# A mixture-of-experts layer: expert weights in three 1-MB loads into pair buffers instead of six 512-KB loads

## The chip, the cores and the metric

The kernel runs on one core of a Trainium2 chip. The metric is the device time of one execution in microseconds (us); shorter is better. Five engines work side by side, each through its own instructions in the order in which the program lists them: TensorE (PE, matrix products), VectorE (DVE), ScalarE (ACT), GpSimd (POOL) and SyncE (SP, which here issues loads and stores). They wait for one another by semaphores. 16 DMA engines move the data.

## The reference, cut to what matters

One layer of an encoder over 1088 tokens (1024 of a prompt and 64 of samples), width 1024: latent attention and a gated convolution, a projection added to the residual, a mixture of 32 experts with the top two of a chosen group, and a gated embedding.

```python
x = x + m @ w_o
h2 = rmsnorm(x, g_ffn).reshape(B * S, D)
# hier_moe: group by top 1 of 4, experts by top 2 of 8 in the group; for each block of tokens of expert eid:
a = xblk @ w1[eid]                       # w1, w3: 1024 x 256 for each expert
b = xblk @ w3[eid]
return (jax.nn.silu(a) * b) @ w2[eid]    # w2: 256 x 1024
...
x = x + hier_moe(h2, ...)
x = x + sigmoid(rmsnorm(x, g_ple) @ w_pg) * (p @ w_ple)
```

All of it is float32. The kernel makes each product from three: an operand is split into a rounded high part and the rest, and high x high, low x high and high x low are summed (`mm3`, lines 64, 65 and 66).

## The kernel before

Up to 740 us run the projections, attention and the convolution; to 860 us the output projection and the router, during which the weights of experts 0 to 4 are fetched. From 860 to about 1192 us stands the **expert stage**. For each of the 32 experts in turn:

- its up to 96 tokens are gathered from `h2d` (L1363, issued by POOL, three experts ahead);
- `x_tr` transposes them on PE (L1373, two banks of four 128-column pieces, 8 instructions), ACT casts the high part `xTh` (one per bank) and DVE makes the low part `xTl`;
- `w13_mm` multiplies by w1 and w3: 24 matmuls of 512 columns (8 pieces of the width, three terms each), called **W** of the expert below;
- `act_` takes the silu on ACT (`sa`, L1391) and the product on DVE (L1392); `a_tr` transposes it with 2 PE instructions (L1399); ACT casts `ath`, DVE makes `atl`;
- `w2_mm` multiplies by w2 in two halves of the width: 12 matmuls, called **Y**; ACT copies each half out (`y`, L1416, two copies); a scatter writes them (L1419).

The weights of an expert lie in memory as six tiles of 128 x 1024 (four of w1 and w3, two of w2). Each is split: ACT casts the high part `weh` (L58), DVE subtracts for the low part `wel` (L61), six of each in flight. So ACT and DVE have six splits per expert, beside the small steps above.

The loads are issued by SP (`e_load`, `w_dma`, L954). Each load is 512 KB with rows of 4 KB, into one of 30 slots of its own; five experts fit, and the load of expert e + 6 is issued behind expert e. A load is held until the load five before it has landed (`DEEP`). Behind the last expert's weights follow `pT` and `wple` (the embedding) and `wpg` (the gate), by the same function.

In the expert stage the order of POOL and SP is the order of the code. The order of PE, DVE and ACT is picked by a scheduler when the program is built: it plays the code through with its own estimates of when an operand will be there, those of the loads among them. Behind the experts come four `ple` products, a loop for experts with more tokens than fit (not entered with this data), and a last stage that PE fills, to the end.

Of the kernel before, what the change touches and what calls it, by code (L numbers as in the profile page):

```python
# [7 lines left out]
F32 = mybir.dt.float32  # L8
# [24 lines left out]
NOV = 22  # L33
NOROW = 2200.0
A2 = 2 * T
DEEP = 5
WARM = 10
WARM0 = 14

# [2 lines left out]
def body(ctx, tc, a):  # L42
# [894 lines left out]
    fxs, fx = opened("flex")  # L937
    NHL, NY = 6, 3

    def slot(j, shape, dt, name):  # L940
        return (fx if j < 24 else fx2[0]).tile(shape, dt, name=name, tag=f"fx{j}", bufs=1)

    fx2 = []
    EP = ((0, 1), (2, 3), (8, 9), (6, 7), (4, 5))

    MCH = ((0, 384), (384, 384), (768, 320))
    mT = [[slot(3 * (2 * (i // 3) + s) + i % 3, [128, KD, 128], F32R, f"mT{i}{s}") for s in range(2 - (i == 8))]
          for i in range(NT)]
    eraw, wsl = {}, {}

    wdma = []
# [6 lines left out]
                              reason="bounded queue")  # L958
        wdma.append(r.ins)

    def e_load(e, js=range(6)):
        for j in js:
            r = slot(3 * EP[e % len(EP)][j // 3] + j % 3, [128, 1024], F32, "eraw")
            w_dma(r, a["we"][e, j])
            eraw[e, j] = r

    ys, yp = opened("ya", bufs=2)
    aTh, aTl = [], []
# [47 lines left out]
    mcf = lgp.tile([128, 32], BF16, name="mcf")  # L1016
    trib = lgp.tile([128, 128], BF16, name="trib")
    oneb = lgp.tile([128, 128], BF16, name="oneb")
    nc.vector.memset(oneb, 1.0)
    nc.vector.memset(lg[:, NT - 1], 0.0)  # L1020
    was, wap = opened("woA", side="right")
    wo = {}
    wos = {k: slot(q, [128, 2, 512], F32R, "wos") for k, q in ((0, 18), (1, 19), (2, 20), (3, 21), (4, 22), (5, 23), (7, 17))}

    def wo_get(k):
        wo[k] = []
# [235 lines left out]
    for i in range(6):  # L1262
        p = i - 1
        o_mm(i, 0, {} if i == 0 else {
            **({0: [(route3, i - 2)]} if i >= 2 else {}), 1: [(o_tr, p, 1), (o_h2, p)], 4: [(o_rt, p, 0, 4)],
            5: [(o_rt, p, 4, 8)], 7: [(o_lg, p), (route1, p)]})
        o_add(i, 0)
        if 1 <= i:
            o_load(i + 1)
        if i == 5:  # L1270
            o_load(7)
        if i == 0:
            e_load(2, range(3))
        if i == 1:
            e_load(2, range(3, 6))
        if i >= 1:
            e_load((i - 1) // 3, ((i - 1) % 3, 3 + (i - 1) % 3))
        o_mm(i, 1, {**({5: [(route2, p)]} if i >= 1 else {}), 6: [(o_tr, i, 0)]})
        o_add(i, 1)
        o_sq(i)  # L1280
# [1 line left out]
                7: [(o_lg, 5), (route1, 5)]})  # L1282
    o_add(6, 0)
    o_load(8)
    e_load(1, (2, 5))
# [5 lines left out]
    e_load(4, (2,))  # L1291
# [4 lines left out]
    e_load(4, (0, 3))  # L1296
# [4 lines left out]
    e_load(4, (5,))  # L1301
# [12 lines left out]
    wpx = {}  # L1314

    def wpx_get(q):
        if q not in wpx:
            wpx[q] = slot(9 + q, [128, 1024], F32R, "wpx")
        return wpx[q]

    def e_hi(e, j):
        if e == NE and j >= NHL:
# [22 lines left out]
        e_hi(e, j)  # L1345
        e_lo(e, j)

    e_load(4, (1, 4))
    route1(7)
    for j in range(6):  # L1350
        e_hi(0, j)
# [141 lines left out]
    for j in range(2, 6):  # L1493
# [4 lines left out]

    PL = {}
    plo = {}  # L1500
    XS = ((2, 5, 8), (20, None, None), (0, 1, 6), (7, 3, 4), (21, 22, 23), (18, 19, None), (2, 5, 8), (20, None, None),
          (0, 1, 6))

    def pl_load(j):
        for k in range(2):
            PL["r", j, k] = slot((24, 27)[j] + k, [128, 1024], F32, "plr")
            w_dma(PL["r", j, k], a[("pT", "wple")[j]][:, k, 0:1024])
        if j == 0:
            PL["r8"] = slot(26, [128, 2, 64], F32, "plr8")
            w_dma(PL["r8"], a["pT"][:, :, NP:])  # L1510

    def pl_split(j, k):
        h = PL["h", j, k] = slot((21, 3)[j] + k, [128, 1024], F32R, "plh")
        l = PL["l", j, k] = slot((0, 6)[j] + k, [128, 1024], F32R, "pll")
        r = PL["r", j, k]
        hi(h, r)
        lo(l, r, h[:])
        if j == k == 0:
            t = PL["c8"] = slot(23, [128, 2, 128], F32R, "plc8")
            hi(t[:, :, 0:64], PL["r8"])  # L1520
            lo(t[:, :, 64:128], PL["r8"], t[:, :, 0:64])
# [88 lines left out]
    with tc.For_i(0, nov, 1) as i:  # L1610
        ev = nc.values_load(ovi[0:1, bass.ds(i + 1, 1)], engines=(mybir.EngineType.SP,), min_val=0, max_val=NE - 1,
                            skip_runtime_bounds_check_because="bounded by a minimum on the chip")
        xgo = op_.tile([128, D], F32, name="xgo", tag="xyo")
        nc.gpsimd.memset(xgo, 0.0)
        rb = op_.tile([128, 128], F32, name="rb")
        V_.tensor_scalar(out=rb, in0=rid, scalar1=bs, scalar2=None, op0=OP.add)
        V_.tensor_scalar(out=bs, in0=bs, scalar1=128.0, scalar2=None, op0=OP.add)
        ps = bank()
        for k in range(2):
            for t in range(NT):  # L1620
                am = op_.tile([128, 128], F32, name="amo", bufs=1)
# [141 lines left out]
def pack(inp):  # L1763
# [107 lines left out]
```

## Time and profile before

| what | value |
|---|---|
| median of 3 runs | 1332.31 us (1332.3 to 1336.3) |
| the profiled execution | 1331.4 us, its span 1329.5 us |
| PE busy | 1268.9 us, 95% of the span |
| DVE busy | 854.9 us, 64% |
| ACT busy | 650.6 us, 49% |
| weights' DMA queue (q1) | 221.86 MB, 47.8% of 16 engines' span |
| the four experts in 1067 to 1106 us | 39.0 us, 9.75 us for each |

The first time is a whole execution's, the span runs from the first to the last instruction; the rest of the table is of the span. A busy share is a mean over stages with different limits: how an engine stands in one stage is read from a window of that stage. PE works through its instructions in order, so a wait on PE delays all behind it; a busy ACT or DVE delays PE only where the row that PE needs stands behind others in their queues.

### The profile page before, as it was taken

How to read it: one execution, taken by the hardware profiler on the slowest of the kernel's cores; microseconds unless marked ns; L12 is line 12 of the kernel's file. 1: busy time of each engine (PE TensorE's matmuls, PEld its weight loads, DVE VectorE, ACT ScalarE, POOL GpSimd, SP SyncE). 2: the span in 40 equal slices, each digit the busy share in tenths (PEclk: the TensorE clock that was granted, in tenths of full speed). 3: DMA queues.
4: the chain of work that ended last, by engine and by line, in shares of the span. 5: the costliest groups of instructions: out<-in, count | busy, mean ns of one | idle time of the engine just before them, and what ended most of it. 6: DMA issues, size and time to landing. Idle time of an engine off the chain costs nothing. (4 is left out here: it accounts for less than half of the span.)

```text
span 1329.5 us, 20478 instructions
## 1 busy us (share of the span) xinstructions
PE 1268.9 (95%) x7255; PEld 1100.2 (83%) x7255; DVE 854.9 (64%) x1652; ACT 650.6 (49%) x1278; POOL 319.4 (24%) x376
## 2 busy tenths in 40 slices
PE   9999999999988999999999999789999999999998
PEld 8999999999978988888998887556766666667886
DVE  6433354336684566766559755689888888884743
ACT  6311242223344455655545211358888888785322
POOL 2000011125653233433315200032222222210310
PEclk9999999999998999999999999989999999999999
DMA  7111398535665524332357755799999999947511
GB/s 271 57 48 48 136 365 307 195 116 165 148 204 189 168 74 135 89 131 74 97 187 264 263 195 213 249 295 358 357 354 349 348 351 343 352 173 279 198 40 56
DMA packets 106777, 273.94 MB, mean 206 GB/s; under 512 B 13729, under 2 KB 42897, under 8 KB 106642
## 3 DMA queue, kind: packets, MB, share of 16 engines
q1 hardware_dynamic: 90544, 221.86, 47.8%
q0 software_dynamic: 15840, 50.68, 11.9%
q8 instruction: 58, 0.95, 0.3%
q14 instruction: 45, 0.37, 0.1%
q10 hardware_dynamic: 290, 0.07, 0.0%
HBM read 212.72 MB, written 67.19 MB: 211 GB/s over the span
## 5 line engine op out<-in xcount | busy, mean ns | idle before, releaser
L61 DVE TENSOR_TENSOR wel<-eraw,weh 128x1024 fp32r<-128x1024 f32 x192 | 228.5, 1220 | 35.6 <-ACT weh L58 33.8
L58 ACT CAST weh<-eraw 128x1024 fp32r<-128x1024 f32 x192 | 195.5, 1054 | 10.9 <-PE bk L66 10.9
L829 POOL TENSOR_TENSOR P<-P,ri 128x128 f32<-128x128 f32 (+8 forms) x72 | 77.2, 1077 | 128.5 <-DVE ri L828 108.9
L65 PE MATMUL bk<-wel,xTh 128*96 128x512 f32 x256 | 103.6, 405 | 2.0 <-DVE wel L61 1.7
L64 PE MATMUL bk<-weh,xTh 128*96 128x512 f32 x256 | 102.3, 400 | 2.4 <-ACT xTh L58 1.7
L66 PE MATMUL bk<-weh,xTl 128*96 128x512 f32 x256 | 102.6, 401 | 0.0
L1419 POOL DMA_INDIRECT Yd<-y,idx x32 | 41.0, 1280 | 234.0 <-ACT y L1416 215.5
L64 PE MATMUL bk<-hTAh,wh 128*128 128x384 f32 x224 | 76.3, 341 | 0.5 <-ACT hTAh L257 0.3
L65 PE MATMUL bk<-hTAl,wh 128*128 128x384 f32 x224 | 76.1, 340 | 0.0
L66 PE MATMUL bk<-hTAh,wl 128*128 128x384 f32 x224 | 75.9, 339 | 0.0
L64 PE MATMUL fg<-hTBh,fw 128*128 128x384 f32 (+1 forms) x224 | 74.5, 333 | 0.3 <-ACT fgm L665 0.2
L66 PE MATMUL fg<-hTBh,fw 128*128 128x384 f32 (+1 forms) x224 | 72.9, 326 | 0.0
L65 PE MATMUL fg<-hTBl,fw 128*128 128x384 f32 (+1 forms) x224 | 72.7, 325 | 0.0
L58 ACT CAST wh<-w_r 128x1024 fp32r<-128x1024 f32 x28 | 29.4, 1051 | 87.5 <-issue 42.4
L64 PE MATMUL bk<-hTBh,wh 128*128 128x384 f32 (+1 forms) x192 | 62.0, 324 | 0.2 <-ACT hTBh L58 0.2
L65 PE MATMUL bk<-hTBl,wh 128*128 128x384 f32 (+1 forms) x192 | 62.0, 323 | 0.0
L66 PE MATMUL bk<-hTBh,wl 128*128 128x384 f32 (+1 forms) x192 | 61.9, 323 | 0.0
L61 DVE TENSOR_TENSOR wl<-w_r,wh 128x1024 fp32r<-128x1024 f32 x28 | 34.3, 1225 | 40.0 <-ACT wh L58 39.9
L65 PEld LDWEIGHTS bk<-wel,xTh 128*96 128x96 f32 x256 | 41.6, 163 | 22.2 <-DVE wel L61 7.9
L64 PE MATMUL bk<-weh,ath 128*96 128x512 f32 x128 | 51.0, 398 | 8.9 <-ACT ath L58 8.8
L815 DVE TENSOR_REDUCE nm<-S 128x1 f32<-128x128 f32 (+8 forms) x72 | 50.8, 706 | 12.3 <-PE S L66 11.2
L64 PEld LDWEIGHTS bk<-weh,xTh 128*96 128x96 f32 x256 | 41.5, 162 | 20.6 <-ACT xTh L58 3.1
(804 smaller groups left out, 3749.7 us busy)
## 6 DMA issues: line engine op xcount, KB each, us to landing
eraw<-in_we_dram SPq DMA_DIRECT2D x192, 512.0 KB
fw<-wsd POOLq DMA_DIRECT2D x32, 512.0 KB, 5.1
w_r<-in_wing_dram SPq DMA_DIRECT2D x28, 512.0 KB
gm_r<-gscr SPq DMA_DIRECT2D x16, 544.0 KB
wsd<-wh SPq DMA_DIRECT2D x16, 512.0 KB
wsd<-wl SPq DMA_DIRECT2D x16, 512.0 KB
xy<-Yd SPq DMA_DIRECT2D x16, 512.0 KB
vd<-V SPq DMA_DIRECT2D x10, 512.0 KB
```

Source lines behind the costliest of these rows:

```text
L58: nc.scalar.copy(dst, src)
L61: (eng or nc.vector).tensor_tensor(out=dst, in0=src, in1=h.bitcast(F32), op=OP.subtract)
L64: r = nc.tensor.matmul(ps, sh, mh, start=first, stop=False)
L65: nc.tensor.matmul(ps, sh, ml, start=False, stop=False)
L66: nc.tensor.matmul(ps, sl, mh, start=False, stop=last)
L815: nc.vector.tensor_reduce(out=nm, in_=s, axis=AX.XY, op=OP.max, negate=True)
L829: nc.gpsimd.tensor_tensor(out=P[:, :nk], in0=P[:, :nk], in1=ri.to_broadcast([128, nk]), op=OP.mult)
L1419: nc.gpsimd.indirect_dma_start(out=Yd[:, :], out_offset=bass.IndirectOffsetOnAxis(ap=col, axis=0), in_=buf, in_offset=None, bounds_check=A ...
```

## The change

The weights lie in memory as three tiles of 128 x 2048 per expert. A load is 1 MB with rows of 8 KB, into one of 15 pair buffers, which hold two of the former slots; the held-back load waits for the one three before it. The embedding's and the gate's weights are loaded as pairs too. The buffers that other stages borrow are renumbered accordingly, and a small tile (`plc8`) gets a place of its own. The number of instructions on PE, DVE, ACT and POOL stays the same; SP has 456 in place of 558.

```diff
-DEEP = 5
+DEEP = 3
...
-    def slot(j, shape, dt, name):
-        return (fx if j < 24 else fx2[0]).tile(shape, dt, name=name, tag=f"fx{j}", bufs=1)
...
-    EP = ((0, 1), (2, 3), (8, 9), (6, 7), (4, 5))
+    EP = ((0, 1, 2), (3, 4, 5), (12, 13, 14), (9, 10, 11), (6, 7, 8))
+
+    def pair(p, dt, name):
+        return (fx if p < 12 else fx2[0]).tile([128, 2, 1024], dt, name=name, tag=f"fx{p}", bufs=1)
...
-    def e_load(e, js=range(6)):
-        for j in js:
-            r = slot(3 * EP[e % len(EP)][j // 3] + j % 3, [128, 1024], F32, "eraw")
-            w_dma(r, a["we"][e, j])
-            eraw[e, j] = r
+    def e_load(e, qs=range(3)):
+        for q in qs:
+            r = pair(EP[e % len(EP)][q], F32, "eraw")
+            w_dma(r, a["we"][e, q].rearrange("p (j n) -> p j n", j=2))
+            for j in range(2):
+                eraw[e, 2 * q + j] = r[:, j]
...
-            e_load((i - 1) // 3, ((i - 1) % 3, 3 + (i - 1) % 3))
+            e_load((i - 1) // 3, ((i - 1) % 3,))
...
     def pl_load(j):
+        r = pair(12 + j, F32, "plr")
+        w_dma(r, a[("pT", "wple")[j]][:, :, 0:1024])
         for k in range(2):
-            PL["r", j, k] = slot((24, 27)[j] + k, [128, 1024], F32, "plr")
-            w_dma(PL["r", j, k], a[("pT", "wple")[j]][:, k, 0:1024])
+            PL["r", j, k] = r[:, k]
...
     def wpg_load(s):
-        for k in range(3 * s, min(3 * s + 3, KD)):
-            eraw[NE, k] = slot(12 + k, [128, 1024], F32, "eraw")
-            w_dma(eraw[NE, k], a["wpg"][:, k])
+        for q in range(*((0, 3), (3, 4))[s]):
+            r = pair((9, 10, 11, 6)[q], F32, "eraw")
+            w_dma(r, a["wpg"][:, 2 * q:2 * q + 2])
+            for j in range(2):
+                eraw[NE, 2 * q + j] = r[:, j]
...
-    A["we"] = np.ascontiguousarray(we.reshape(32, 128, 6, 1024).transpose(0, 2, 1, 3))
+    A["we"] = np.ascontiguousarray(we.reshape(32, 128, 3, 2048).transpose(0, 2, 1, 3))
```

Up to the W of expert 16 the rows of PE, DVE and ACT stand as before. From there on the scheduler picks another order, with a pattern that repeats every four experts in both kernels. Three places show it.

**ACT, from the splits of w2 of expert 20 on, before.** `weh_11940` and `weh_11968` are these splits, `weh_11987` and on of expert 21 (`weh<-eraw` is a split), `y_12011` is the output of expert 19, `xTh0_12039` and `xTh1_12068` are the casts of expert 21's tokens, `sa_12077` is the silu of expert 20:

```order
L58 CAST weh_11940<-eraw_11420 128x1024
L58 CAST weh_11968<-eraw_11422 128x1024
L58 CAST xTh0_12039<-bk_12041 128x384
L58 CAST weh_11987<-eraw_11524 128x1024
L1416 COPY y_12011<-bk_12012 96x512
L58 CAST weh_12031<-eraw_11526 128x1024
L1416 COPY y_12011<-bk_12020 96x512
L58 CAST weh_12035<-eraw_11528 128x1024
L58 CAST xTh1_12068<-bk_12070 128x384
L58 CAST weh_12048<-eraw_11530 128x1024
L1391 ACTIVATE sa_12077<-bk_11991 96x256
```

The first cast stands ahead of four splits and both copies of `y`. The same place now: `weh_11820` and the four behind it are expert 21's splits, `y_11844` the output of expert 19, `xTh0_11872` and `xTh1_11901` expert 21's tokens:

```order
L58 CAST weh_11820<-eraw_11387 128x1024
L58 CAST weh_11864<-eraw_11387 128x1024
L1394 ACTIVATE sa_11910<-bk_11824 96x256
L1419 COPY y_11844<-bk_11845 96x512
L58 CAST weh_11868<-eraw_11389 128x1024
L1419 COPY y_11844<-bk_11853 96x512
L58 CAST weh_11881<-eraw_11389 128x1024
L58 CAST xTh0_11872<-bk_11874 128x384
L58 CAST xTh1_11901<-bk_11903 128x384
L58 CAST ath_11940<-bk_11937 128x192
```

Both casts moved behind both copies of `y` and four splits of expert 21.

**PE at the W of expert 21, before.** `bk_12020` is the second half of Y of expert 19, `bk_12041` and `bk_12070` take the transposed tokens of expert 21, `bk_11991` is W of expert 20:

```order
L64 MATMUL bk_12012<-weh_11828,ath_12001 96x512
L65 MATMUL bk_12012<-wel_11829,ath_12001 96x512
L64 MATMUL bk_12020<-weh_11828,ath_12001 96x512
L65 MATMUL bk_12020<-wel_11829,ath_12001 96x512
L1373 MATMUL bk_12041<-ident_58,xg0_9662 128x96 x4
L1373 MATMUL bk_12070<-ident_58,xg0_9662 128x96 x4
L65 MATMUL bk_11991<-wel_11924,xTh1_11956 96x512
```

The transposes stand amid W of expert 20. There now (`bk_11853` is the second half of Y of expert 19, `bk_11874` and `bk_11903` the tokens of expert 21, `bk_11930` its W, `bk_11937` the transposed activations of expert 20, `bk_11951` its Y):

```order
L66 MATMUL bk_11853<-weh_11701,atl_11835 96x512
L1376 MATMUL bk_11874<-ident_58,xg0_9621 128x96 x4
L1376 MATMUL bk_11903<-ident_58,xg0_9621 128x96 x4
L64 MATMUL bk_11930<-weh_11820,xTh0_11872 96x512
L65 MATMUL bk_11930<-wel_11821,xTh0_11872 96x512
L1402 MATMUL bk_11937<-ident_58,sa_11910 128x96 x2
L64 MATMUL bk_11951<-weh_11779,ath_11940 96x512
L65 MATMUL bk_11951<-wel_11780,ath_11940 96x512
L64 MATMUL bk_11959<-weh_11779,ath_11940 96x512
```

Before, 19 more matmuls of PE (W of expert 20 and Y of expert 19) stand between these transposes and the W that needs their casts. Now none does.

**ACT behind the first copy for expert 22, now.** `y_11950` is the output of expert 20, `weh_11926` and on are splits of expert 22, `sa_12016` is the silu of expert 21, `xTh0_11978` and `xTh1_12007` are the casts of expert 22's tokens:

```order
L58 CAST weh_11926<-eraw_11493 128x1024
L1419 COPY y_11950<-bk_11951 96x512
L58 CAST weh_11970<-eraw_11493 128x1024
L1419 COPY y_11950<-bk_11959 96x512
L58 CAST weh_11974<-eraw_11495 128x1024
L58 CAST weh_11987<-eraw_11495 128x1024
L1394 ACTIVATE sa_12016<-bk_11930 96x256
L58 CAST xTh0_11978<-bk_11980 128x384
L58 CAST xTh1_12007<-bk_12009 128x384
```

The casts are the last two rows. Before (`weh_12099` and on are of expert 22, `xTh0_12151` the cast of its tokens, `y_12123` the output of expert 20):

```order
L58 CAST weh_12099<-eraw_11636 128x1024
L58 CAST weh_12143<-eraw_11638 128x1024
L58 CAST ath_12113<-bk_12110 128x192
L1391 ACTIVATE sa_12189<-bk_12103 96x256
L58 CAST xTh0_12151<-bk_12153 128x384
L58 CAST xTh1_12180<-bk_12182 128x384
L1416 COPY y_12123<-bk_12124 96x512
L58 CAST weh_12147<-eraw_11640 128x1024
L1416 COPY y_12123<-bk_12132 96x512
L58 CAST weh_12160<-eraw_11642 128x1024
```

Here, too, the casts moved behind the copies and three splits. On PE, the transposes of expert 22 are now ended right ahead of its W, with 4 matmuls of expert 21 between Y of expert 20 and them. For expert 23 PE has 4, 4, 2 and 4 instructions (W of expert 22, half of the transposes, W, the other half) between Y of expert 21 and the W, and ACT has `y`, split, `y`, split, `xTh0`. For expert 24, ACT has the casts ahead of the copies.

Toward the end, ACT now has the two splits of `pT` (`plh`) behind `ath` of expert 28; before, they stand behind the splits of expert 31:

```order
L58 CAST xTh1_12749<-bk_12751 128x384
L58 CAST ath_12779<-bk_12776 128x192
L58 CAST plh_12959<-plr_12553 128x1024 x2
L58 CAST weh_12733<-eraw_12239 128x1024
L58 CAST weh_12761<-eraw_12239 128x1024
L58 CAST plc8_7586<-late_12555 128x2x64
L58 CAST weh_12765<-eraw_12341 128x1024
L1419 COPY y_12789<-bk_12790 96x512
```

The two splits of `pT` stand ahead of the last two splits of expert 29.

## Rows read from the trace of the kernel before

**Rows 1.** Windows: us, busy of PE, PEld, DVE, ACT, POOL, clock, DMA share, GB/s.

```profile
1067.00:1106.00 39.00, 37.58 (x186) 26.29 (x185) 34.26 (x41) 32.58 (x49) 9.85 (x8) 1.00 1.00 347
1145.00:1203.00 58.00, 53.61 (x242) 37.03 (x240) 44.97 (x53) 47.23 (x68) 8.34 (x7) 1.00 0.60 209
```

**Rows 2.** What PE waited for in 1067 to 1106: us, times, longest us.

```profile
PE bk L64 <- ACT ath L58: 1.2, 1, 1.2
PE bk L64 <- ACT xTh L58: 0.2, 1, 0.2
```

**Rows 3.** Timeline of PE in 1085 to 1089: start us, us, engine, line, out<-in, [idle].

```profile
1085.31 0.82 PE L1373 MATMUL bk<-ident,xg 96*128 96x96 f32 x8
...
1086.38 0.47 PE L64 MATMUL bk<-weh,xTh 128*96 128x512 f32 x1 [0.24 <-ACT xTh L58]
...
1086.92 0.39 PE L66 MATMUL bk<-weh,atl 128*96 128x512 f32 x1
...
1088.77 0.33 PE L1399 MATMUL bk<-ident,sa 96*128 96x96 f32 x2
```

**Rows 4.** Timeline of ACT over the same stretch.

```profile
1085.84 0.86 ACT L58 CAST xTh<-bk 128x384 fp32r<-128x384 f32 x2 [1.31 <-PE bk L1373]
1088.04 0.58 ACT L1416 COPY y<-bk 96x512 f32<-96x512 f32 x1 [1.33 <-PE bk L66]
1088.52 1.05 ACT L58 CAST weh<-eraw 128x1024 fp32r<-128x1024 f32 x1
1089.47 0.58 ACT L1416 COPY y<-bk 96x512 f32<-96x512 f32 x1
1089.94 1.05 ACT L58 CAST weh<-eraw 128x1024 fp32r<-128x1024 f32 x1
```

**Rows 5.** Groups by line, 911 to 1106: busy us, mean ns, idle before.

```profile
L61 DVE TENSOR_TENSOR wel<-eraw,weh 128x1024 fp32r<-128x1024 f32 x121 | 144.0, 1221 | 23.7 <-ACT weh L58 22.7 <-DMA eraw<-in_we_dram 0.2
...
L61 DVE TENSOR_TENSOR xTl<-bk,xTh 128x384 fp32r<-128x384 f32 x40 | 20.7, 548 | 0.0
...
L1392 DVE TENSOR_TENSOR sa<-sa,bk 96x256 f32<-96x256 f32 x20 | 8.2, 408 | 0.0
...
L1391 ACT ACTIVATE sa<-bk 96x256 f32<-96x256 f32 x20 | 7.6, 380 | 0.0
```

**Rows 6.** What PE waited for in 1145 to 1203.

```profile
PE bk L65 <- DVE wel L61: 1.7, 3, 0.8
PE bk L1399 <- DVE sa L1392: 1.2, 1, 1.2
PE bk L64 <- ACT weh L58: 0.7, 2, 0.5
PE bk L64 <- ACT ath L58: 0.4, 1, 0.4
```

**Rows 7.** What PE waited for in 870 to 911.

```profile
PE bk L1373 <- DMA xg<-h2d,idx: 3.0, 2, 2.0
```

**Rows 8.** Timeline of POOL at the first gather.

```profile
865.73 1.14 POOL L1363 DMA_INDIRECT xg<-h2d,idx  x1 [5.30 <-DMA eraw<-in_we_dram]
```

**Rows 9.** DMA queues in 900 to 1150: packets, MB, share of 16 engines.

```profile
q1 hardware_dynamic: 20269, 73.83, 83.5%
```

**Rows 10.** Timeline of SP in 1150 to 1176.

```profile
1158.02 3.14 SPq L954 DMA_DIRECT2D plr<-in_pT_dram  x3
1161.92 2.33 SPq L954 DMA_DIRECT2D plr<-in_wple_dram  x2
1165.20 6.30 SPq L954 DMA_DIRECT2D eraw<-in_wpg_dram  x6
```

**Rows 11.** Timeline of ACT, DVE and PE at the loop after the experts.

```profile
1202.72 1.11 ACT L1536 COPY plo<-bk 128x512 f32<-128x512 f32 x2
...
1202.90 1.28 DVE L1338 SCALAR_TENSOR_TENSOR wel<-eraw,gplc,weh 128x1024 fp32r<-128x1024 f32 x1 [0.72 <-ACT weh L1330]
...
1205.08 0.80 PE L64 MATMUL bk<-plh 128*128 128x512 f32 x1 [2.14 <-DVEq L1610]
```

More of the change, by code (lines that the diff above doesn't have):

```diff
@@ L938, in body @@
     NHL, NY = 6, 3
-    def slot(j, shape, dt, name):
-        return (fx if j < 24 else fx2[0]).tile(shape, dt, name=name, tag=f"fx{j}", bufs=1)
     fx2 = []
-    EP = ((0, 1), (2, 3), (8, 9), (6, 7), (4, 5))
+    EP = ((0, 1, 2), (3, 4, 5), (12, 13, 14), (9, 10, 11), (6, 7, 8))
+    def pair(p, dt, name):
+        return (fx if p < 12 else fx2[0]).tile([128, 2, 1024], dt, name=name, tag=f"fx{p}", bufs=1)
     MCH = ((0, 384), (384, 384), (768, 320))
-    mT = [[slot(3 * (2 * (i // 3) + s) + i % 3, [128, KD, 128], F32R, f"mT{i}{s}") for s in range(2 - (i == 8))]
-          for i in range(NT)]
+    mTp = [pair(i, F32R, f"mT{i}") for i in range(NT)]
+    mT = [[mTp[i][:, q].rearrange("p (k n) -> p k n", k=KD) for q in range(2 - (i == 8))] for i in range(NT)]
     eraw, wsl = {}, {}
@@ L1018, in body @@
     oneb = lgp.tile([128, 128], BF16, name="oneb")
+    plc8 = lgp.tile([128, 2, 128], F32R, name="plc8")
     nc.vector.memset(oneb, 1.0)
@@ L1022, in body @@
     wo = {}
-    wos = {k: slot(q, [128, 2, 512], F32R, "wos") for k, q in ((0, 18), (1, 19), (2, 20), (3, 21), (4, 22), (5, 23), (7, 17))}
+    wosp = [pair(9 + q, F32R, "wos") for q in range(3)]
+    wos = {k: wosp[k // 2][:, k % 2].rearrange("p (s n) -> p s n", s=2) for k in range(6)}
+    wos[7] = mTp[8][:, 1].rearrange("p (s n) -> p s n", s=2)
     def wo_get(k):
@@ L1272, in body @@
         if i == 0:
-            e_load(2, range(3))
+            e_load(2, (0, 1))
         if i == 1:
-            e_load(2, range(3, 6))
+            e_load(2, (2,))
         if i >= 1:
-            e_load((i - 1) // 3, ((i - 1) % 3, 3 + (i - 1) % 3))
+            e_load((i - 1) // 3, ((i - 1) % 3,))
         o_mm(i, 1, {**({5: [(route2, p)]} if i >= 1 else {}), 6: [(o_tr, i, 0)]})
@@ L1284, in body @@
     o_load(8)
-    e_load(1, (2, 5))
+    e_load(1, (2,))
     o_mm(8, 0, {5: [(route2, 5)]})
@@ L1290, in body @@
     o_sq(8)
-    e_load(4, (2,))
     o_mm(6, 1, {1: [(o_tr, 8, 1), (o_h2, 8)], 3: [(o_rt, 8, 0, 8)], 4: [(o_lg, 8), (route1, 8)],
@@ L1295, in body @@
     o_sq(6)
-    e_load(4, (0, 3))
+    e_load(4, (0,))
     o_mm(7, 0, {0: [(o_tr, 6, 1)], 1: [(route2, 8), (o_h2, 6)], 2: [(o_rt, 6, 0, 8)], 3: [(route3, 8)],
@@ L1300, in body @@
     e_load(3)
-    e_load(4, (5,))
+    e_load(4, (2,))
     route1b(6)
@@ L1316, in wpx_get @@
     def wpx_get(q):
-        if q not in wpx:
-            wpx[q] = slot(9 + q, [128, 1024], F32R, "wpx")
-        return wpx[q]
+        if q // 2 not in wpx:
+            wpx[q // 2] = pair(9 + q // 2, F32R, "wpx")
+        return wpx[q // 2][:, q % 2]
     def e_hi(e, j):
@@ L1346, in e_split @@
         e_lo(e, j)
-    e_load(4, (1, 4))
+    e_load(4, (1,))
     route1(7)
@@ L1500, in body, with half @@
     plo = {}
-    XS = ((2, 5, 8), (20, None, None), (0, 1, 6), (7, 3, 4), (21, 22, 23), (18, 19, None), (2, 5, 8), (20, None, None),
-          (0, 1, 6))
+    XS = (((2, 0), (2, 1), (5, 1)), ((14, 1), None, None), ((0, 0), (0, 1), (1, 0)), ((1, 1), (7, 0), (7, 1)),
+          ((8, 0), (8, 1), (14, 0)), ((6, 0), (6, 1), None), ((2, 0), (2, 1), (5, 1)), ((14, 1), None, None),
+          ((0, 0), (0, 1), (1, 0)))
+    own = {}
+    def half(p, q):
+        if p not in own:
+            own[p] = pair(p, F32, "late")
+        return own[p][:, q]
     def pl_load(j):
+        r = pair(12 + j, F32, "plr")
+        w_dma(r, a[("pT", "wple")[j]][:, :, 0:1024])
         for k in range(2):
-            PL["r", j, k] = slot((24, 27)[j] + k, [128, 1024], F32, "plr")
-            w_dma(PL["r", j, k], a[("pT", "wple")[j]][:, k, 0:1024])
+            PL["r", j, k] = r[:, k]
         if j == 0:
-            PL["r8"] = slot(26, [128, 2, 64], F32, "plr8")
+            PL["r8"] = half(14, 0)[:, 0:128].rearrange("p (k n) -> p k n", k=2)
             w_dma(PL["r8"], a["pT"][:, :, NP:])
     def pl_split(j, k):
-        h = PL["h", j, k] = slot((21, 3)[j] + k, [128, 1024], F32R, "plh")
-        l = PL["l", j, k] = slot((0, 6)[j] + k, [128, 1024], F32R, "pll")
+        if k == 0:
+            PL["hl", j] = [pair((7, 0)[j] + q, F32R, "pl" + "hl"[q]) for q in range(2)]
+        h = PL["h", j, k] = PL["hl", j][0][:, k]
+        l = PL["l", j, k] = PL["hl", j][1][:, k]
         r = PL["r", j, k]
         hi(h, r)
-        lo(l, r, h[:])
+        lo(l, r, h)
         if j == k == 0:
-            t = PL["c8"] = slot(23, [128, 2, 128], F32R, "plc8")
+            t = PL["c8"] = plc8
             hi(t[:, :, 0:64], PL["r8"])
@@ L1523, in ple @@
     def ple(i):
-        t = plo[i] = slot((24, 27, 15)[i // 3] + i % 3, [128, D], F32, "plo")
+        t = plo[i] = half((12, 13, 3, 4, 5)[i // 2], i % 2)
         r0 = 128 * i
@@ L1551, in late @@
         elif e == NE - 5:
-            wpg_load(0), wpg_load(1)
+            wpg_load(0)
     order = ExitStack()
@@ L1631, in body @@
             r = load(op_, [128, 512],
-                     a["we"][bass.ds(ev, 1), k // 2, :, 512 * (k % 2):512 * (k % 2) + 512].rearrange("o p n -> p (o n)"),
+                     a["we"][bass.ds(ev, 1), k // 4, :, 512 * (k % 4):512 * (k % 4) + 512].rearrange("o p n -> p (o n)"),
                      "ov", 1)
@@ L1643, in body @@
             for b in range(2):
-                c = slice(512 * b, 512 * b + 512)
-                r = load(op_, [128, 512], a["we"][bass.ds(ev, 1), 4 + j, :, c].rearrange("o p n -> p (o n)"), "ov", 1)
+                c = slice(1024 * j + 512 * b, 1024 * j + 512 * b + 512)
+                r = load(op_, [128, 512], a["we"][bass.ds(ev, 1), 2, :, c].rearrange("o p n -> p (o n)"), "ov", 1)
                 wh, wl_ = split(op_, r, [128, 512], "ovs", 1)
@@ L1655, in f_x @@
     def f_x(i, p=None):
-        XY[i] = [fp.tile([128, D], F32, name=f"xy{k}{i % 2}") if q is None else slot(q, [128, D], F32, "xy")
+        XY[i] = [fp.tile([128, D], F32, name=f"xy{k}{i % 2}") if q is None else half(*q)
                  for k, q in enumerate(XS[i])]
@@ L1723, in body @@
     f_x(0), f_y(0)
-    wpg_load(2)
+    wpg_load(1)
     f_x(1), f_y(1)
```

## The prediction

> **What bounds the kernel now.** I read the windows by stage first, then what PE waited for in them, then the timelines of PE and ACT at one hand-over. In the expert stage PE is busy 37.58 of 39.0 us for four experts, 186 instructions [rows 1]. The windows around it repeat these numbers, so a period of four experts takes 39.0 us. PE waits only twice in a period that the list shows, 1.2 us for `ath` and 0.2 us for `xTh` [rows 2], so 1.4 us a period is what PE loses. The DMA engines are busy all the time there (share 1.00, 347 GB/s) [rows 1], and the weights' queue has 83.5% of it [rows 9]. But nothing waits for them: DVE sat idle 0.2 us for a weight tile in 911 to 1106 against 22.7 us for ACT's cast [rows 5]. So the weights arrive ahead of use, and PE's order with ACT's beside it sets the time. ACT is busy 32.58 of 39.0 us and DVE 34.26 [rows 1]: neither is the bound, but neither can be late for long, since ACT works its list in order and a cast that PE needs may stand behind splits that nobody needs yet.
>
> **The loads themselves.** The bytes are the same; 512-KB loads become 1-MB loads, 102 instructions fewer on SP. [...] In the steady stage this is worth nothing, since nothing waits for weights [rows 2, 5]. [...] I take 0 for the steady stage.
>
> **The start of the stage.** The first gather waited 5.30 us, which the profile puts to weight loads in flight [rows 8], and PE waited 3.0 us for two gathers [rows 7]. With 3 MB allowed in flight instead of 2.5 MB, the store of the last tokens, which the gather needs, has up to 0.5 MB more ahead of it, 1.4 us at 347 GB/s [rows 1]. Bounds 0 and +1.4; I take +0.7, the middle, as nothing in the rows is nearer to either.
>
> **The new order, from expert 17 on.** This is the large term. I take durations from a hand-over of before and put them in the new order. Call c the start of the first `y` copy, 1088.04 [rows 4]. PE's next instruction behind the last matmul of Y starts at 1088.77, at c + 0.73. Eight matmuls take 1088.77 - 1086.92 = 1.85 us, 0.23 each. Eight transposes take 1086.38 - 1085.31 less the 0.24 waited, 0.83, and four 0.42 [rows 3]. From the start of the `xTh` cast to the W that it feeds 1086.38 - 1085.84 = 0.54 [rows 3, 4]. On ACT a copy takes 0.48 to the next start, a split 0.95 [rows 4], a silu about 0.28 (0.38 less the 0.1 by which starts overlap) [rows 4, 5].
>
> *Expert 21 and each fourth after it:* PE could begin W at c + 0.73 + 0.83 = 1.56. ACT has copy, split, copy, split ahead of the cast, 0.48 + 0.95 + 0.47 + 0.95 = 2.85, and W starts at 3.39. PE waits 1.83. Two matmuls and two transposes later Y wants `ath`, behind the second cast of the tokens: about another 0.5 (PE's two transposes end at c + 4.07, and cast and start take about what they take for `xTh`). Together 2.3.
>
> *Expert 22:* four matmuls of W stand between, so PE is free at c + 0.73 + 0.92 + 0.83 = 2.48. ACT has copy, split, copy, two splits and the silu ahead: 2.85 + 0.95 + 0.28 = 4.08, W starts at 4.62: 2.14. DVE follows: the second split behind the copy ends at c + 2.95, two low parts of 1.22 and the product of 0.41 [rows 5] make 5.8, and PE wants the product at 5.08: 0.7. `xTl`, 0.55 behind it, comes some 0.3 late. Together 3.1.
>
> *Expert 23:* PE is free at c + 0.73 + 0.92 + 0.42 + 0.46 + 0.42 = 2.95, W starts at 3.39: 0.44. `xTl` needs the low part of the split before it (2.95 + 1.22) and 0.55 of its own, 4.72, where PE wants it at 3.85: 0.87. Together 1.3.
>
> *Expert 24:* the casts are ahead of the copies; 0.
>
> A period then holds 2.3 + 3.1 + 1.3 = 6.7 us of waits in place of 1.4, +5.3. Experts 17 to 28 are three periods: **+16**. Bounds: if only the waits for the first cast counted, 1.83 + 2.14 + 0.44 - 1.4 = 3.0 a period, +9; if each of the three places also waited for a buffer of the splits, which Y of two experts before holds to its last half (up to the 0.9 us of four matmuls, row as above), +2.7 a period, +24.
>
> **The end of the stage.** Experts 29 to 31 repeat the three places, 6.7 us, and DVE and ACT have the four splits of `pT` and `wple` among theirs; a pair of low parts, 2.4 us [rows 5], stands ahead of the product of expert 29, of which I count 1.4 us as not hidden. Against that stand the waits that before had there, 1.7 + 1.2 + 0.7 + 0.4 = 4.0 [rows 6]. I take 8.1 - 4.0 = +4.1; bounds 0 and +8. At the loop DVE ended at 1204.18 and ACT at 1203.83, and PE went on at 1205.08 after 2.14 us [rows 11]; the new order has DVE's last piece earlier, so ACT is next: -0.35. The last stage starts with the same data in place; I cost it at 0.
>
> **Sum against the profiled execution, 1331.4:** 0.7 + 16 + 4.1 - 0.35 = +20.5, so 1351.9. The median is 0.9 above that execution: **1353**. By the bounds +8.7 to +33: 1341 to 1365.
>
> **Rivals.**
> *Faster: loads of 1 MB land sooner and the waits at both ends go.* If my reading of the order were wrong and the new order hid all casts, the 4.0 us at the end [rows 6], 0.35 at the loop and about 1 of the 3.0 at the start [rows 7] could go: 1332.3 - 5.3 = 1327. If the 1.4 us of three periods went too, 1323. For it: the waits are there. Against it: DMA is already at 347 GB/s with a share of 1.00 [rows 1], and weights are waited for nowhere in the steady stage [rows 5]; above all the three places would have to show no wait. [...] Chance 0.14.
>
> *No change.* The scheduler puts an instruction where its operands are to be had, and ACT has 6.4 us of idle time in a period [rows 1]; if ACT ran far enough ahead that splits stand ready before the copies, the casts would come in time. Against: in the three places the splits stand *behind* the copies in the list, and cannot run ahead of them. With +0.7 - 0.35 at the ends: 1333. That the 8-KB rows are moved in pieces as before, so that the loads change nothing, gives the same time only if the order did nothing either; the order comes with it all the same. Chance 0.12.
>
> *Slower by another way: the embedding's weights are wanted too early.* ACT now splits `pT` right behind `ath` of expert 28. At before's pace that is two periods and one expert behind 1067, 1067 + 78.0 + 9.75 = 1154.8, about 1156.5 with the few instructions of the next expert that stand ahead. `pT` is issued from 1158.0, and the load five later starts at 1165.2, which is when the first half had landed [rows 10]. ACT would stand 8.7 us, with the splits of expert 29 behind it and PE behind these: 1332.3 + 8.7 = 1341. It decides only where the order's waits do not delay expert 29 by as much; with them, the +16 has ACT arrive at about 1172, and this wait is gone. Chance 0.08.
>
> **How the numbers follow.** The forecast has 0.66, and with the early demand slower has 0.74; no change (within 0.3%, some 4 us, about what a measurement here can tell) 0.12; faster 0.14. Leaving out the faster case and the last few hundredths above, the range goes from 1331, which takes in most of no change, to 1366.
>
> **What would show it.** In the changed kernel's trace the four experts from 21 on should take 44 to 45 us instead of 39.0, with PE waiting some 4 us in a period for `xTh`, and 1 to 2 for low parts and products of DVE; up to expert 16 it should stay at 39.0. If a period stays at 39 to 40, the reading of the order is wrong; if DVE or ACT wait for loads by microseconds, the weights' pace decides, and not the order; if PE waits at about 1156 for splits behind `plh`, it is the early demand.

## The result, and the profile after

The changed kernel takes 1367.65 us (median of 4 runs, 1366.51 to 1368.73) against 1332.78 us before (4 runs): a ratio of 1.026, 95% interval 1.0242 to 1.0278. It is slower, as forecast, but by 34.9 us and not by 20.5; the time lies 1.65 us above the range. The profiled execution took 1367.24 us, with a span of 1365.1 us against 1329.5.

Windows of the kernel after, columns as in [rows 1] (us, busy of PE, PEld, DVE, ACT, POOL, PE clock, DMA share, GB/s):

```profile
989.00:1028.00 39.00, 37.58 (x186) 26.30 (x185) 34.27 (x41) 32.59 (x50) 10.57 (x8) 1.00 1.00 354
1028.00:1067.00 39.00, 33.00 (x144) 22.18 (x143) 28.66 (x33) 26.66 (x40) 8.95 (x8) 0.91 0.97 331
1067.00:1106.00 39.00, 33.92 (x152) 23.42 (x151) 28.24 (x34) 26.97 (x39) 7.20 (x6) 0.91 0.99 364
```

Up to 1028 all is as in [rows 1]: 186 matmuls in 39 us. Then expert 17 comes, and 39 us hold only 144 to 152 matmuls. DMA is as busy as before. The clock column (the granted clock of TensorE, as a share of full speed) is the one to see: 0.91 instead of 1.00.

What PE waited for in 1072 to 1116, to be held against [rows 2]:

```profile
PE bk L64 <- ACT xTh L58: 4.7, 3, 2.1
PE bk L66 <- DVE xTl L61: 0.6, 1, 0.6
PE bk L1402 <- DVE sa L1395: 0.4, 1, 0.4
PE bk L64 <- ACT ath L58: 0.4, 1, 0.4
```

The waits are 6.1 us where the forecast had 6.7, and they stand at the instructions that it named. But they are not all. Timeline of PE at the W of expert 17, the first of the three places, and the start of the next two W of the same kind (experts 21 and 25):

```profile
1035.77 0.82 PE L1376 MATMUL bk<-ident,xg 96*128 96x96 f32 x8
1038.71 0.58 PE L64 MATMUL bk<-weh,xTh 128*96 128x512 f32 x1 [2.12 <-ACT xTh L58]
1039.09 0.63 PE L65 MATMUL bk<-wel,xTh 128*96 128x512 f32 x1
...
1040.99 0.63 PE L65 MATMUL bk<-wel,ath 128*96 128x512 f32 x1
1041.42 0.63 PE L64 MATMUL bk<-weh,ath 128*96 128x512 f32 x1
...
1042.27 0.44 PE L66 MATMUL bk<-weh,xTl 128*96 128x512 f32 x1
1042.55 0.39 PE L64 MATMUL bk<-weh,xTh 128*96 128x512 f32 x1
...
1085.66 0.47 PE L64 MATMUL bk<-weh,xTh 128*96 128x512 f32 x1 [2.13 <-ACT xTh L58]
...
1133.00 0.47 PE L64 MATMUL bk<-weh,xTh 128*96 128x512 f32 x1 [2.13 <-ACT xTh L58]
```

Behind the wait of 2.12 us the matmuls take 0.63 us and follow each other at 0.43; from 1042.5 on they take 0.39 and follow at 0.23. A period from expert 21 to 25 is 1133.00 - 1085.66 = 47.34 us, 8.34 more than before. 6.1 - 1.4 = 4.7 of it are waits. Of the other 3.6 most are matmuls at the lower clock (2.7, by a run below). The windows of the same places (ahead of the place above, behind its wait, and behind the one at expert 18) show the granted clock:

```profile
1030.00:1036.00 6.00, 6.00 (x29) 4.23 (x28) 5.31 (x6) 4.54 (x7) 1.28 (x2) 1.00 0.95 326
1038.80:1042.20 3.40, 2.99 (x8) 1.84 (x9) 1.99 (x4) 0.56 (x2) 1.95 (x2) 0.52 0.95 302
1052.30:1055.50 3.20, 2.95 (x8) 1.68 (x9) 2.27 (x5) 0.55 (x2) 0.36 (x1) 0.54 1.01 378
```

The clock is 1.00 ahead of the first wait, and 0.52 and 0.54 behind the two waits, where the matmuls follow each other at 0.43 us.

ACT over the first place shows why PE waits, and has the order that was read from the built program: copy, split, copy, split, then the casts (compare [rows 4]):

```profile
1035.34 0.57 ACT L1419 COPY y<-bk 96x512 f32<-96x512 f32 x1
1035.81 1.05 ACT L58 CAST weh<-eraw 128x1024 fp32r<-128x1024 f32 x1
1036.75 0.59 ACT L1419 COPY y<-bk 96x512 f32<-96x512 f32 x1
1037.23 1.05 ACT L58 CAST weh<-eraw 128x1024 fp32r<-128x1024 f32 x1
1038.18 0.86 ACT L58 CAST xTh<-bk 128x384 fp32r<-128x384 f32 x2
```

The end, 1160 to 1250, answers to [rows 6]:

```profile
PE bk L64 <- ACT xTh L58: 5.6, 3, 2.1
PE bk L64 <- ACT ath L58: 2.8, 2, 2.4
PE bk L64 <- issue: 2.1, 1, 2.1
PE bk L1402 <- DVE sa L1395: 1.7, 1, 1.7
PE bk L66 <- DVE xTl L61: 1.3, 2, 0.7
```

Without the loop's 2.1 these are 11.4 us, against 4.0 before.

**Where the 35.6 us of span went.** Ahead of the new order the kernel after is early by 1.4 us: the last of the waits of 1.19 us for `ath` that both kernels have there ends at 1004.91 after and at 1006.31 before. Most of that are the waits for gathers, 1.9 us where [rows 7] has 3.0. Experts 17 to 28 are three periods of +8.34: +25.0. At the loop PE went on at 1239.71, where [rows 11] has 1205.08: +34.6 in all, so 29 to 31 and the products behind them are 34.6 - 25.0 + 1.4 = +11.0. The rest, +1.0, is in the last stage.

### The profile page after: what moved, and what is told of

It reads as the page before. It is cut to its first block, busy times and chain, and to the rows that moved or that the text cites. A ratio compares the mean times of both kernels' runs of the same rounds, so it can differ in the third digit from the quotient of the medians.

```text
span 1365.1 us, 20201 instructions
## 1 busy us (share of the span) xinstructions
PE 1283.5 (94%) x7255; PEld 1109.2 (81%) x7255; DVE 856.5 (63%) x1652; ACT 653.1 (48%) x1278; POOL 320.8 (24%) x376
## 5 line engine op out<-in xcount | busy, mean ns | idle before, releaser
L64 PE MATMUL bk<-weh,xTh 128*96 128x512 f32 x256 | 106.5, 416 | 20.9 <-ACT xTh L58 20.9
L66 PE MATMUL bk<-weh,xTl 128*96 128x512 f32 x256 | 107.6, 420 | 2.9 <-DVE xTl L61 2.8
L58 ACT CAST wh<-w_r 128x1024 fp32r<-128x1024 f32 x28 | 29.4, 1050 | 89.0 <-issue 44.6
L66 PEld LDWEIGHTS bk<-weh,xTl 128*96 128x96 f32 x256 | 43.7, 171 | 23.1 <-DVE xTl L61 7.0
```

The source lines that it names most:

```text
L58: nc.scalar.copy(dst, src)
L64: r = nc.tensor.matmul(ps, sh, mh, start=first, stop=False)
L66: nc.tensor.matmul(ps, sl, mh, start=False, stop=last)
```

## The experiments

Two theories stood against each other at first: the **order** that the scheduler picked (with the clock as a part of it or not), and the **loads**. For most runs the order of PE, DVE and ACT in the expert stage was written out as three lists, which the code then follows; with the lists of a kernel's own order its instructions stand as in that kernel. In a list `H.21.2` is ACT's split of tile 2 of expert 21 and `L` DVE's part of it, `XH.21.0` and `XL` the casts of its tokens, `YC.19.0` the copy of a half of Y of expert 19, `SA` the silu, `SM` the product, `AH` the cast `ath`, `H.32` and `PH` the splits of the gate's and the embedding's weights; on PE, `W.21x2` are two matmuls of W, `X` transposes of tokens, `A` of activations, `P` products of the embedding.

**Order of before, loads of after.**

```diff
-    order.enter_context(tc.manual_schedule(engines={ET.Pool, ET.SP}))
+    order.enter_context(tc.manual_schedule(engines={ET.PE, ET.DVE, ET.Activation, ET.Pool, ET.SP}))
...
-ACT, as scheduled: H.20.4 H.20.5 H.21.0 H.21.1 SA.20 YC.19.0 H.21.2 YC.19.1 H.21.3 XH.21.0 XH.21.1 AH.20
+ACT, as a list:    H.20.4 H.20.5 XH.21.0 H.21.0 YC.19.0 H.21.1 YC.19.1 H.21.2 XH.21.1 H.21.3 SA.20
```

> The changed kernel's loads (three of 1 MB) with the order of PE, DVE and ACT in the expert stage written out as the kernel before has it. Theory 'order': the loads cost nothing, so 1331 us (the 1.5 us that the stage's start gained stay), and four experts take 39.0 us. Rival 'loads': the 1-MB loads slow the stage themselves, then 1360 or more, with four experts over 45 us.

Measured: 1329.88 us (10 runs), ratio 0.9985 to before (0.9976 to 0.9995). A window of 39 us holds what it held before, at a clock of 1.00:

```profile
1028.00:1067.00 39.00, 37.57 (x185) 26.21 (x184) 34.24 (x40) 32.57 (x49) 8.21 (x9) 1.00 0.96 337
```

All of the loss is gone with the loads still at 1 MB. What is left in favour of the loads is about 2 us, which the interval hardly parts from nothing.

**Loads of before, order of after.** The same two sides, exchanged: the kernel before, with the changed kernel's lists up to the last expert.

> The kernel before with its six loads of 512 KB, but the changed kernel's order of PE, DVE and ACT in the expert stage, up to the last expert's products; behind these the order of before. Theory 'order': four experts take 47.3 us from expert 17 on, as in the changed kernel, +25 us for experts 17 to 28 and +6 to +8 for 29 to 31: 1363 to 1367 us. Rival 'loads': 1333 us, 39.0 us for four experts.

Measured: 1368.0 us (4 runs), ratio 1.0271 (1.024 to 1.0303). What PE waited for in 1077 to 1124 is, to the tenth, what it waited for in the kernel after:

```profile
PE bk L1678 <- ACT xTh L138: 4.7, 3, 2.1
PE bk L1678 <- DVE xTl L141: 0.6, 1, 0.6
PE bk L1691 <- DVE sa L1788: 0.4, 1, 0.4
PE bk L1701 <- ACT ath L138: 0.4, 1, 0.4
```

The order alone makes the loss; the loads by themselves do nothing to it. What remains was why it is 35 us and not 20.

**PE kept busy in the waits.** Nine matmuls whose results nobody reads stand where PE waits 2.1 us, at 8 places:

```diff
-X.21.0x4 X.21.1x4 W.21x2 A.20x2
+X.21.0x4 X.21.1x4 D.21x9 W.21x2 A.20x2
...
+            nc.tensor.matmul(rp.s[t], wsl[t[1], 0][0][:, 0:128], wsl[t[1], 0][0][:, 0:512], start=True, stop=True)
```

> The changed kernel with its own order, written out, and nine idle matmuls of 512 columns on PE (results not used) ahead of the first matmul of w1 and w3 of experts 17, 18, 21, 22, 25, 26, 29 and 30, where PE waits 2.1 us. Theory 'clock': PE is not idle there, the granted clock stays at its upper level, and the 8 matmuls behind each wait that now take 0.43 us each take 0.23: some 1.7 us for each place, 8 places, 1354 to 1356 us, with more instructions. Rival 'waits alone': the clock is set by something else; 1367 us or a little more.

Measured: 1354.75 us (4 runs), ratio 1.0171 (1.0146 to 1.0196): 12.9 us faster than the changed kernel, with 72 matmuls more. The same 3.4 us behind the start of W of expert 17, which here is at 1036.24 (the window that stood at 0.52 above):

```profile
1036.30:1039.70 3.40, 2.99 (x14) 2.01 (x15) 1.97 (x4) 0.63 (x3) 2.43 (x2) 1.00 0.93 311
```

ACT's order is the same, and the work that PE waits for comes no sooner: W of expert 29 starts 2.95 us behind the start of its transposes in both kernels (1177.69 to 1180.64 after, 1167.27 to 1170.22 here). PE only has something to do meanwhile. So the 12.9 us are the price of the clock behind the waits, 1.6 us for each of the 8 places on the mean. A period, from `ath` of expert 20 to that of expert 24, is 44.67 us here and 47.34 in the kernel after (1086.94 to 1134.28):

```profile
1082.17 0.47 PE L1717 MATMUL bk<-weh,ath 128*96 128x512 f32 x1 [0.41 <-ACT ath L137]
...
1126.84 0.47 PE L1717 MATMUL bk<-weh,ath 128*96 128x512 f32 x1 [0.41 <-ACT ath L137]
```

That is 2.67 us a period, 1.3 a place. Expert 30's place costs more than the mean: there a second wait, of 1.67 us, stands behind the first, and the matmuls are slow for 5.4 us (1197.23 to 1202.66).

**The casts ahead of the splits.** PE's order stays. On ACT and DVE the casts of the next tokens stand ahead of two splits:

```diff
-ACT: SA.20 YC.19.0 H.21.2 YC.19.1 H.21.3 XH.21.0 XH.21.1 AH.20
+ACT: SA.20 YC.19.0 YC.19.1 XH.21.0 XH.21.1 H.21.2 H.21.3 AH.20
```

> The changed kernel, PE's order unchanged; on ACT and DVE only the casts of the next expert's tokens (and the silu, the product and the copy ahead of them) stand ahead of two splits, at experts 17 to 19, 21 to 23, 25 to 27, 29 and 30. Theory 'the cast stands behind splits': the waits of 2.1 us shrink to about 0.4, the low-part waits go, the clock stays up, four experts take 39 to 40 us; with the end as it was 1338 to 1345 us. Rival 'PE's order is at fault' (transposes right ahead of the product that needs them): four experts still over 45 us, above 1360.

Measured: 1347.13 us, ratio 1.0106 (1.0084 to 1.0129). In the steady stage the theory holds. PE starts the W of experts 21 and 25 at:

```profile
1078.59 0.47 PE L1694 MATMUL bk<-weh,xTh 128*96 128x512 f32 x1 [0.39 <-ACT xTh L137]
1081.07 0.47 PE L1717 MATMUL bk<-weh,ath 128*96 128x512 f32 x1 [1.61 <-ACT ath L137]
...
1119.01 0.47 PE L1694 MATMUL bk<-weh,xTh 128*96 128x512 f32 x1 [0.38 <-ACT xTh L137]
1121.50 0.74 PE L1717 MATMUL bk<-weh,ath 128*96 128x512 f32 x1 [1.61 <-ACT ath L137]
```

A period is 1119.01 - 1078.59 = 40.4 us; the wait of 2.1 is 0.39, and `ath` is what is late next, 1.61. The expectation of 39 to 40 left that out. And at the end a new wait came, first on ACT, then on PE:

```profile
1168.75 2.00 ACT L137 CAST plh<-plr 128x1024 fp32r<-128x1024 f32 x2 [5.38 <-DMA plr<-in_pT_dram]
...
1176.39 0.74 PE L1694 MATMUL bk<-weh,xTh 128*96 128x512 f32 x1 [4.19 <-ACT xTh L137]
```

This is the third rival of the prediction, the embedding's weights wanted too early: it was hidden in the changed kernel since the waits had made expert 29 late (ACT comes to this split at 1181.76 there and does not wait), and it appears once they are gone.

**The last expert's cast ahead of the gate's splits.** In the changed kernel ACT has four splits of the gate's weights ahead of `ath` of the last expert.

```diff
-ACT: AH.30 H.32.0 SA.31 H.32.1 YC.30.0 H.32.2 YC.30.1 H.32.3 AH.31
+ACT: AH.30 SA.31 YC.30.0 YC.30.1 AH.31 H.32.0 H.32.1 H.32.2 H.32.3
```

> The changed kernel with its order, but the first four splits of the gate's weights stand behind the cast of the last expert's activations on ACT and DVE, not ahead of it. Theory: the wait of 2.4 us for that cast and the slow matmuls behind it go: 1363 to 1364 us against 1367.6. Rival: the wait only moves to the next thing, 1367.

Measured: 1363.91 us, ratio 1.0216 (1.0195 to 1.0237), 3.7 us less than the changed kernel. The wait of 2.4 is 0.72, and the matmuls behind it are no longer slow:

```profile
1220.69 0.47 PE L1717 MATMUL bk<-weh,ath 128*96 128x512 f32 x1 [0.72 <-ACT ath L137]
```

**The end as before, in the changed kernel's order.** All splits of the embedding and the gate stand behind those of expert 31.

```diff
-ACT: XH.29.1 AH.28 PH.0.0 PH.0.1 H.29.4 ... AH.30 H.32.0 SA.31 H.32.1 YC.30.0
+ACT: XH.29.1 AH.28 H.29.4 ... AH.30 YC.30.0 YC.30.1 PH.0.0 SA.31 PH.0.1 P8 AH.31
-PE: Y.31.0x2 Y.31.1x2 P.0.0x6 ... Y.31.0x4 Y.31.1x4
+PE: Y.31.0x2 Y.31.1x2 Y.31.0x4 Y.31.1x4 P.0.0 P.0.1
```

> The changed kernel with its own order, but the splits of the embedding's and the gate's weights stand behind the last expert's splits again, as in the kernel before. Theory: the wait of 2.4 us for the last expert's transposed activations and 1.3 us of the wait of 1.7 us for the product of expert 29 go, and the slow matmuls behind them: 1362 to 1364 us, against 1367.6. Rival: the splits then stand in the way of the last products themselves, and the time stays at 1367.

Measured: 1368.66 us, ratio 1.0268 (1.0251 to 1.0285). That is a miss; no gain. The two waits that were to go went, but a split and two late copies now stood ahead of the last silu, and PE waited for its product:

```profile
1223.81 0.39 PE L1708 MATMUL bk<-ident,sa 96*128 96x96 f32 x2 [3.20 <-DVE sa L1805]
```

The run set a piece of one order into another, and the piece made its own wait. Why the same piece is not late in the order of before was not tested. (The run with the loads of before had these same three lists: 1368.0 and 1368.66 us, so the size of the loads made no difference there either.)

**Casts first, and an end that suits them.** The casts as above, and at the end the silu of expert 31 ahead of the first split of the embedding.

```diff
-ACT: AH.28 PH.0.0 PH.0.1 H.29.4 ... H.32.0 SA.31 H.32.1 YC.30.0 H.32.2 YC.30.1 H.32.3 AH.31
+ACT: AH.28 H.29.4 ... SA.31 PH.0.0 YC.30.0 YC.30.1 AH.31 PH.0.1 P8 PH.1.0 PH.1.1 YC.31.0 H.32.0
```

> As the run with the casts ahead of two splits, and the splits of the embedding's and the gate's weights stand behind the last expert's splits and its silu, as far as in the kernel before. Theory 'early demand': ACT's wait of 5.4 us for the embedding's weights goes, and with it PE's waits of 4.2 us (cast), 1.7 us (product) and 2.4 us (the last expert's cast) and their slow matmuls: 1333 to 1338 us, which is the kernel before with the waits of 1.2 and 1.6 us that PE's order keeps. Rival: other waits take their place, over 1343.

Measured: 1338.36 us (7 runs), ratio 1.0049 (1.0033 to 1.0065), 8.8 us less than with the casts alone (some 7 of it when each is set against the times of before that were taken beside it), at the edge of what was expected. Its profiled execution was the slowest of its runs, with 5 us of that ahead of the expert stage, so only its list of PE's waits from 1028 on is of use:

```profile
PE bk L1718 <- ACT ath L138: 7.2, 5, 1.6
PE bk L1695 <- ACT xTh L138: 3.8, 9, 1.3
PE bk L144 <- DVEq L1875: 2.1, 1, 2.1
```

No wait is over 2.1, and the one for the product is gone. With PE's order untouched but for the embedding's products, which stand behind the last expert's, some 28 of the 35 us came back.

**An order of our own, with either size of load.** Each expert alike, the transposes of tokens well ahead of their use and the casts ahead of the splits:

```diff
-PE: W.21x2 A.20x2 Y.20.0x2 Y.20.1x2 W.21x18 Y.20.0x4 Y.20.1x4 W.21x4 X.22.0x4 X.22.1x4 W.22x2
+PE: W.21x6 A.20x2 W.21x5 Y.20.0x2 Y.20.1x2 W.21x2 X.22.0x4 W.21x5 X.22.1x4 W.21x6 Y.20.0x4 Y.20.1x4 W.22x6
-ACT: SA.20 YC.19.0 H.21.2 YC.19.1 H.21.3 XH.21.0 XH.21.1 AH.20
+ACT: H.21.0 XH.21.0 H.21.1 H.20.4 SA.20 YC.19.0 H.21.2 YC.19.1 XH.21.1 AH.20 H.21.3
```

> The changed kernel's loads with an order of our own for PE, DVE and ACT: each expert alike, transposed activations after 6 matmuls of the next expert's w1 and w3, four products of w2 after 11, the next tokens' transposes after 13 and 18, the other eight products of w2 at the end, and the casts of the tokens ahead of the splits. Theory 'order': PE's 36 matmuls and 10 transposes alone take 9.4 us in place of 9.75, 11 us for 32 experts, and the waits at the end (4.0 us) mostly go: 1314 to 1320 us. Rival 'weights': at 10.9 us of loading for each expert the lead of five experts is used up before the last, and DVE or ACT wait for loads: 1322 to 1330.

> The same order of our own with the six 512-KB loads of the kernel before. Theory 'order': the same time as with the 1-MB loads, within 2 us. Rival 'loads': where weights become late, the 1-MB loads are faster by more than 2 us.

Measured: 1324.02 us with 1-MB loads, ratio 0.993 (0.9913 to 0.9948), and 1323.09 us with 512-KB loads, ratio 0.9912 (0.9894 to 0.9931). Both beat the kernel before, and neither reaches 1314 to 1320. As far as the traces show, the reason is the rival that was written down: in both, ACT now waits for weights. With 1-MB loads PE is busy all the time in 900 to 1000, and for 84.3 of 90 us in 1100 to 1190:

```profile
900.00:1000.00 100.00, 100.00 (x503) 71.72 (x502) 93.00 (x109) 89.20 (x132) 33.40 (x22) 1.00 1.00 357
1100.00:1190.00 90.00, 84.29 (x386) 56.42 (x385) 70.94 (x83) 71.37 (x107) 21.77 (x13) 1.00 0.91 327
```

No run gave these orders more lead to show it by experiment. What ACT waited for: the first row is of the 1-MB loads, the second of the 512-KB loads, 872 to 1190:

```profile
ACT weh L141 <- DMA eraw<-in_we_dram: 24.5, 11, 3.4
```

```profile
ACT weh L141 <- DMA eraw<-in_we_dram: 20.0, 20, 2.7
```

And here, where loading is the limit, the larger loads are no faster. In 1050 to 1150 the weights' queue moved 28.87 MB (1-MB loads) and 28.55 MB (512-KB loads):

```profile
q1 hardware_dynamic: 3966, 28.87, 81.8%
```

```profile
q1 hardware_dynamic: 7842, 28.55, 82.2%
```

Half the packets, 1% more bytes, and 0.9 us between the two times, less than the spread of the runs.

## Why the prediction was right or wrong

**What bounds the stage: right.** PE's order with ACT's beside it. The exchange of orders and loads shows it from both sides (1329.88 and 1368.0).

**The loads, 0 in the steady stage: right.** Three pairs of kernels have one order and differ in the loads: with 1-MB loads against 512-KB loads 1329.88 to 1332.93 us (the times of before taken beside it), 1368.66 to 1368.0, and 1324.02 to 1323.09. Where loading was the limit, 512-KB loads moved 28.55 MB in 100 us and 1-MB loads 28.87. The 39-us windows shown have 347 GB/s [rows 1] with 512-KB loads and 331 to 364 with 1-MB loads; no run shows what sets them.

**The start, +0.7: wrong in sign, small.** PE waited 1.1 us less for gathers. This is no property of the loads that we could show: over the profiled executions of all these kernels the sum of these waits was 2.6 to 3.7 us in the three with 512-KB loads and 1.1 to 3.5 in the eight with 1-MB loads. The two overlap.

**The new order, +16 for experts 17 to 28: the step that failed.** The waits were right: 6.1 us a period where 6.7 were worked out, each at its instruction (2.13, 2.12 and 0.46 for `xTh` where 1.83, 2.14 and 0.44 stood). What was left out is what a wait does to the matmuls behind it. The sum took every matmul at the 0.23 us of a stage in which PE never waited longer than 1.2, and priced a wait at its own length. Behind each wait of 2.1 us in experts 17 to 28 the matmuls followed each other at 0.43 us for 3 to 4 us (the clock was 0.52 and 0.54 in the two windows above), which cost 2.67 us a period by the filled run. So four experts took 47.34 us and not 44 to 45, and the three periods cost 25.0 us: 3 x 4.7 = 14.1 are waits, 3 x 2.67 = 8.0 are the clock, and some 2.9 are in neither. The filled run has that part too (44.67 - 39.0 - 4.7 is 1.0 a period, with the clock up); where it lies was not followed up. The sign of the clock stood among the rows that the prediction itself used: in [rows 11] PE goes on after 2.14 us of waiting with a matmul of 0.80 us, where [rows 3] has 0.47 and 0.39; the clock in 1205.1 to 1208.5 of before was 0.52. The row was read for its time and not for its duration. The upper bound, +24 for this term, took in waits for buffers, which did not come, and had no term for the clock. That the measured 25.0 lies only just above it is luck.

**The end, +4.1: mis-sized, +11.0.** The wait for the product of expert 29 came somewhat shorter than priced (1.67, where 0.7 and 1.4 were counted), the slow matmuls at two more of the 8 places are 3.2 at the mean price, and one wait was not seen: the gate's splits ahead of the last expert's `ath`, 2.36 us and the slow matmuls behind it, 3.7 together by its own run. 4.1 + 3.2 + 3.7 = 11.0. (That the sum meets the measured figure to the tenth is chance: it takes the forecast's 4.1 for the other waits.) That wait could have been read from the order as the others were; the last expert's rows were not walked through.

**The loop, -0.35: wrong.** PE's wait there was 2.14 us in both kernels, counted from PE's own end (1237.57 to 1239.71 after). DVE's last piece ended 1.2 us behind PE before and 2.6 us ahead of it after, and nothing was gained: the end of DVE's work did not set this wait.

**The last stage, 0:** +1.0, not followed up.

**The rivals.** "Faster" needed the three places to show no wait, and they show one each (2.1, 2.1 and 0.46 us for `xTh`). "No change" needed ACT to be so far ahead that the casts come in time, and they did not. "Wanted too early" was real and stood behind the order's waits, as the prediction said: with the waits removed it cost ACT 5.4 us and PE 4.2. The forecast time was too low because the mechanism of the forecast was priced without its second half, not because another one decided.

## What to carry to other kernels

When a change lets a scheduler order the engines anew, walk the list of the engine that feeds the bound one: here PE waited 2.13 us for a short cast behind two splits of 0.95 that nobody needed yet, and 0.39 with the cast ahead of them. Price a wait on TensorE with the matmuls behind it, which here cost 1.3 us more for each wait of 2.1 in the steady stage: look in the trace for waits as long as the one that is forecast, and read how long the next ten or so matmuls take behind each. Look at several, since not every such wait was followed by slow ones here. Before making loads larger, look whether anything waits for a load; here nothing did in the steady stage [rows 2, 5], and the order that the scheduler derived from the new loads cost 35 us, while an order written out gained 9 with either size.

## What was not expected of the hardware

- Idle matmuls that fill a wait made the kernel 12.9 us faster (1367.65 to 1354.75), with the work that was waited for no earlier.
- In the kernel after, the clock fell behind every one of the 8 waits of 2.1 us, at once or up to 1.6 us behind the wait's end (2.8 at expert 30), and some 6 to 8 matmuls were slow (12 at expert 30). Runs that kept these waits show it too: with the end as before the matmuls took 0.63 us behind the waits of 2.13 and 2.12 at experts 29 and 30, with the last cast ahead of the gate's splits behind that of 2.13 at expert 30, and with the loads of before and the order of after the clock was 0.91 in 1028 to 1067. But the length of the wait alone does not tell. In the run with the casts first, the clock fell behind one of four waits of 1.61 us (0.74 us for the next matmul, at 1121.50) and not behind the others (0.47 at 1081.07 and at 1163.42; the first of the four stands in 1028 to 1067, where the clock was 1.00). Behind the wait of 2.4 us for the last expert's `ath` of the same run it did not fall either, where in the kernel after it fell behind that of 2.36 (matmuls of 0.63 us from 1223.26 on). First the run with the casts first, then the kernel after:

```profile
1204.90:1208.50 3.60, 3.58 (x16) 2.85 (x17) 1.34 (x2) 0.59 (x1) 0.35 (x1) 1.00 0.26 74
```

```profile
1222.00:1225.60 3.60, 3.58 (x11) 2.80 (x12) 1.35 (x2) 0.00 (x0) 0.36 (x1) 0.67 0.26 74
```

  Behind a wait of 1.3 us at expert 31, with a further one of 0.65 behind it, the matmuls stayed at 0.39 to 0.48 us in the kernel after (a clock of 1.00 in 1209.8 to 1216), in the filled run and in the run with the last cast ahead of the gate's splits; behind the six waits of 1.19 in 911 to 1145 of before the next matmul took 0.47 us each time.
- Beside loads with 8-KB rows the gathers landed later. Gathers in 900 to 1020, their number and the median from issue to landing in us: before, then after.

```profile
xg<-h2d,idx POOLq DMA_INDIRECT x12, 8.2
```

```profile
xg<-h2d,idx POOLq DMA_INDIRECT x12, 10.2
```

  With the order of after and 512-KB loads it was 8.7. With the order of our own it was 9.3 with 512-KB loads (10 gathers in 1050 to 1150) and 10.9 with 1-MB loads (9); the kernel after has 10.0 there. The weights' queue moved 35.84 MB in 9836 packets in 900 to 1020 before, and 36.52 MB in 5025 after; what holds the gathers back is not in the traces. The gathers are issued three experts ahead, 29 us at 9.75 us for each, and no wait for one stands in the list of 1072 to 1116, so it cost nothing there.
